# Column blocks of an input projection walked to and fro, with the turning block kept in PSUM and the order re-planned

## The chip, the cores and the metric

One core of one Trainium2 chip runs the whole program. The time is device microseconds of one execution; the kernel before has a median of 1818.54 us over three runs (1816.66 to 1821.82).

## The reference: one hybrid attention and RG-LRU layer

A layer of width 4096 works on 256 latent tokens (`x`) and 256 context tokens (`ctx`), all in float32. Cut to what matters here:

```python
shift, scale, gate = split(silu(c) @ w_ada + b_ada, 3)      # w_ada: 4096 x 12288; for c and for c_ctx
h_x = rmsnorm(x, norm_w) * (1 + scale_x) + shift_x          # the same for ctx with c_ctx
q, k, v, ga, xl, gl = split(h @ w_in)                       # w_in: 4096 x 9216
att = gqa(rope(qknorm(q)), [rope(k_x), k_ctx], [v_x, v_ctx])
lru = sum over 2 directions of an RG-LRU scan of conv(xl), the context scanned first
x + gate * (concat(rmsnorm(att) * silu(ga), rmsnorm(lru) * silu(gl)) @ w_out)   # w_out: 4096 x 4096
```

Only the latent stream is returned, so of the context only k, v and xl are needed.

## The kernel before: stages, groups and the planned order

**Numbers.** A product of two float32 matrices is made of three TensorE passes: each operand is split into a rounded part `hi` and a rest `lo`, and `hi*hi + hi*lo + lo*hi` is summed in PSUM. For a weight that means a load of 512 KB into one of six `raw` buffers (SP issues these loads, L298), a cast to `hi` on ScalarE (ACT, L646) and a subtraction to `lo` on VectorE (DVE, L650), which frees the raw buffer.

**First stage (to about 747 us).** Everything that both token streams need: column blocks `k`, `v`, `l0` to `l3` of w_in, 512 columns each, against 32 tiles of 128 rows of w_in (k-tiles). The h of a k-tile exists only after the modulation of its 128 channels is known, and this needs the whole height of w_ada for these columns. So the k-tiles are taken in 11 groups of 1, 1, 2, 2, 2, 4, 4, 4, 4, 4, 4 (`FIRST`, `groups`). In a group, `group_pieces` goes through the six blocks in the same order each time; of a block there are four tiles (latent or context, two halves of tokens), each summed in one of four PSUM banks `pm` over the k-tiles of this group. At a block's end `accum_task` moves the four tiles to accumulators in SBUF: a copy on DVE in group 0 (L693), an add on DVE afterwards (L695). That makes 24 evictions a group. Group 0 runs its blocks twice, first for the latent tokens, then for the context.

`mod_tasks` computes shift and scale of the next group's channels, for both c and c_ctx. Its loads of w_ada go to one of two engines by quads (four of the 32 rows a partition holds): TensorE with 32 output rows (L485), or DVE, a multiply-add for each row and vector (L473, L475), summed over partitions at the end by two small matmuls (`fold`, L498). `MOD_V` says how many of eight quads of shift and of scale are DVE's; in the groups of four k-tiles it is none of the shift's and seven of the scale's, in the small groups none. `coeff_tasks` and `prep_tasks` then scale, transpose (L597), modulate (ACT, L607 and L608) and split h (DVE, L617).

**Around it.** The start loads x in eight slices (`load_stream`, L364), whose squares ACT sums (L385); then w_ada for group 0, then ctx. Small parameters and the rope tables come through POOL's DMA queue: `load_params` (L373 to L380) fills rows of one tile `par`, cleared by one memset (L333), and `rope_tasks` (L433 to L443) loads the cosine and sine table into a slot `u`, the broadcast norm weight into `rope` (two DMAs at L435, eight at L440), and multiplies them. `params(1, 2)` transposes the late parameters and `decay` makes the LRU's decay from them with some 25 small DVE instructions (L410 to L424). After the first stage come the query blocks with attention, the two gates beside 16 LRU heads (conv, gates L1227 to L1229, scans L1270 and L1271), and the output projection; DVE sums w_ada for the output gate (L846) along the way, and l0 to l3 are spilled to DRAM through POOL (L893).

**The order.** Each engine runs its instructions in the order in which the program issues them. That order is made at build time by `Plan`: a task has a list of engines with costs, dependencies, PSUM and SBUF slots to take and give, a place in the main chain (`pos`) and often a place before which it may not start (`nb`). `order` simulates the engines with those costs and issues whatever could start first, by `pos` where several could. `LAT` is the lag between engines; a load is reckoned at 1.3 us before it, `LOAD` = 1.6 us for it and `LOAD_LAT` = 0.5 us after. A wait that the plan doesn't know stops an engine, and all behind it. DMAs that depend on nothing start as soon as their queue gets to them, whatever their place in the plan.

## Time and profile before

| | us |
|---|---|
| median of three runs | 1818.54 |
| the profiled execution: its time | 1821.06 |
| its span | 1819.2 |
| busy: PE / DVE / ACT / POOL | 1732.4 / 1419.1 / 854.8 / 68.0 |
| first main matmul (L738) starts | 41.6 |
| last group of the first stage starts | 677.7 |
| mean HBM traffic over the span | 247 GB/s |

PE is TensorE, SP the engine that issues the loads. PE's busy time is modelled, since its matmuls overlap, so a busy PE is not yet a PE at its peak; waits and their releasers tell more. An answer by windows gives busy us of each engine in a stretch, with the number of its instructions, the granted share of TensorE's clock, the busy share of the 16 DMA engines and the traffic. Groups 0, 1, 4 and 6 of the first stage start their main matmuls at 41.6, 76, 208.7 and 353.4 us.

### The profile page before, as it was taken

To read this page: it belongs to the slowest core of one execution; us is meant where nothing else is said; L and a number is where in the kernel's file an instruction comes from. 1 tells how busy PE (TensorE), PEld (TensorE's weight loads), DVE (VectorE), ACT (ScalarE), POOL (GpSimd) and SP (SyncE) were. 2 spreads that over 40 slices of the span, in tenths; PEclk is the share of its full clock that TensorE was granted. 3 is DMA by queue.
4 is the path that set the end of the run, shared out by engine and by line. 5 is a ranking of instruction groups with operands and counts; after the bars stand their busy time and mean duration, and the time that the engine had idled before them with its cause. 6 is when DMAs were issued, how large, how long until landed. Compare 5 with 4: busy or idle time off the path is not lost.

```text
span 1819.2 us, 25705 instructions
## 1 busy us (share of the span) xinstructions
PE 1732.4 (95%) x9709; PEld 1386.6 (76%) x9709; DVE 1419.1 (78%) x2000; ACT 854.8 (47%) x1258; POOL 68.0 (4%) x111
## 2 busy tenths in 40 slices
PE   2989989999999999999999999999999999999998
PEld 1556646676767677887777899999999988888887
DVE  1665988998989797556799778987996997777774
ACT  4422221323323133367776866758667643333332
POOL 2000000000000000200000000000000000000000
PEclk9999999999999999999999999999999999999999
DMA  9989988788886975863466447765875798989893
GB/s 284 337 277 309 323 307 297 259 269 278 280 297 226 329 244 175 248 197 116 141 206 223 148 125 240 243 204 174 278 251 159 220 322 298 313 296 315 300 307 117
DMA packets 286331, 451.80 MB, mean 248 GB/s; under 512 B 15136, under 2 KB 122512, under 8 KB 285696
## 3 DMA queue, kind: packets, MB, share of 16 engines
q1 hardware_dynamic: 279392, 428.43, 71.8%
q0 software_dynamic: 6816, 21.74, 4.0%
q8 instruction: 76, 1.25, 0.3%
q14 instruction: 47, 0.39, 0.1%
HBM read 441.72 MB, written 8.39 MB: 247 GB/s over the span
## 4 chain that ended last, share of the span: by engine, by line
issue 43%; PE 39%; DVE 12%; ACT 3%; DMA 2%; POOL 0%; DVEq 0%; ACTq 0%; POOLq 0%
PE pm L915 8%; PE pm L916 8%; PE pm L914 8%; DVE lo L650 4%; PE pm L939 4%; PE pm L938 4%; PE pm L940 4%; DVE ga L846 2%; PE po L1104 1%; ACT hi L646 1%; DVE h L1270 1%; DVE h L1271 1%; PE pe L1066 1%; DVE u L1204 1%; PE pt L1090 1%
## 5 line engine op out<-in xcount | busy, mean ns | idle before, releaser
L646 ACT CAST hi<-raw 128x1024 fp32r<-128x1024 f32 x416 | 435.7, 1048 | 716.8 <-PE pm L740 336.9
L650 DVE TENSOR_TENSOR lo<-raw,hi 128x1024 fp32r<-128x1024 f32 x416 | 506.9, 1221 | 165.2 <-ACT hi L646 162.4
L738 PE MATMUL pm<-hi,h 128*128 128x512 f32 x768 | 316.5, 412 | 10.9 <-DVE a L695 8.7
L914 PE MATMUL pm<-hi,h 128*128 128x512 f32 x768 | 308.5, 402 | 0.0
L740 PE MATMUL pm<-hi,h 128*128 128x512 f32 x768 | 302.2, 394 | 3.5 <-DVE h L617 3.5
L739 PE MATMUL pm<-lo,h 128*128 128x512 f32 x768 | 302.0, 393 | 0.8 <-DVE lo L650 0.8
L915 PE MATMUL pm<-lo,h 128*128 128x512 f32 x768 | 299.7, 390 | 1.6 <-DVE lo L650 1.6
L916 PE MATMUL pm<-hi,h 128*128 128x512 f32 x768 | 299.4, 390 | 0.0
L938 PE MATMUL pm<-h,hi 128*128 128x256 f32 x1024 | 293.7, 287 | 0.0
L940 PE MATMUL pm<-h,lo 128*128 128x256 f32 x1024 | 290.7, 284 | 0.8 <-DVE lo L650 0.8
L939 PE MATMUL pm<-h,hi 128*128 128x256 f32 x1024 | 290.2, 283 | 0.0
L738 PEld LDWEIGHTS pm<-hi,h 128*128 128x128 f32 x768 | 145.4, 189 | 104.0 <-issue 41.0
L695 DVE TENSOR_TENSOR a<-pm,a 128x512 f32<-128x512 f32 x240 | 159.4, 685 | 67.9 <-PE pm L740 67.9
L939 PEld LDWEIGHTS pm<-h,hi 128*128 128x128 f32 x1024 | 197.0, 192 | 1.7 <-issue 0.7
L938 PEld LDWEIGHTS pm<-h,hi 128*128 128x128 f32 x1024 | 196.9, 192 | 1.7 <-issue 0.7
L940 PEld LDWEIGHTS pm<-h,lo 128*128 128x128 f32 x1024 | 196.8, 192 | 1.4 <-DVE lo L650 1.4
L846 DVE SCALAR_TENSOR_TENSOR ga<-raw,sc,ga 128x512 f32<-128x512 f32 x248 | 185.8, 749 | 8.1 <-DMA raw<-in_w_ada_dram 3.2
L740 PEld LDWEIGHTS pm<-hi,h 128*128 128x128 f32 x768 | 145.5, 189 | 36.0 <-DVE h L617 3.9
L915 PEld LDWEIGHTS pm<-lo,h 128*128 128x128 f32 x768 | 144.4, 188 | 35.0 <-DVE lo L650 3.5
L914 PEld LDWEIGHTS pm<-hi,h 128*128 128x128 f32 x768 | 144.3, 188 | 31.3 <-issue 3.1
L916 PEld LDWEIGHTS pm<-hi,h 128*128 128x128 f32 x768 | 144.1, 188 | 30.4
L739 PEld LDWEIGHTS pm<-lo,h 128*128 128x128 f32 x768 | 145.7, 190 | 27.2 <-DVE lo L650 1.3
(191 smaller groups left out, 1700.7 us busy)
## 6 DMA issues: line engine op xcount, KB each, us to landing
raw<-in_w_ada_dram SPq DMA_DIRECT2D x384, 512.0 KB, 5.5
raw<-in_w_in_dram SPq DMA_DIRECT2D x288, 512.0 KB, 4.8
raw<-in_w_out_dram SPq DMA_DIRECT2D x128, 512.0 KB, 5.3
h<-in_x_dram SPq DMA_DIRECT2D x8, 512.0 KB, 8.8
h<-in_ctx_dram SPq DMA_DIRECT2D x8, 512.0 KB, 10.7
xl_d<-a POOLq DMA_DIRECT2D x4, 1024.0 KB, 6.7
xin<-xl_d POOLq DMA_DIRECT2D x16, 256.0 KB, 4.6
a<-in_x_dram POOLq DMA_DIRECT2D x8, 512.0 KB, 6.7
```

The lines of the kernel that those rows point to most:

```text
L646: S.copy(d["hi"], raw)
L650: V.tensor_tensor(out=d["lo"], in0=d["raw"], in1=d["hi"].bitcast(F32), op=ALU.subtract)
L738: T.matmul(ps[s, t], hi, wh, start=f, stop=False)
L739: T.matmul(ps[s, t], hi, wl, start=False, stop=False)
L740: T.matmul(ps[s, t], lo, wh, start=False, stop=e)
L846: V.scalar_tensor_tensor(out=d["acc"], in0=w[:, i], scalar=s_, in1=d["acc"], op0=ALU.mult, op1=ALU.add)
L914: T.matmul(ps[t], hi, wh, start=f, stop=False)
L915: T.matmul(ps[t], hi, wl, start=False, stop=False)
L916: T.matmul(ps[t], lo, wh, start=False, stop=e)
L938: T.matmul(o, wh, hi, start=f, stop=False, skip_group_check=True)
L939: T.matmul(o, wh, lo, start=False, stop=False, skip_group_check=True)
L940: T.matmul(o, wl, hi, start=False, stop=e, skip_group_check=True)
```

## The change

Odd groups go through the blocks backwards, so the last block of a group is the first of the next. Its four tiles are not evicted at that turn; the sum goes on in the same four PSUM banks (at the first turn only the context's two tiles, since the latent ones were done earlier). The first eviction of each of the 24 tiles is now a copy on ACT instead of DVE. `MOD_V` gives DVE two and three of the scale's quads in groups 3 and 4 (none before), five in group 5 (seven before). `load_params` runs behind a memset of its two rows of `par` at 0.6 of a unit after the first main matmul, and the key's rope loads behind a one-element memset of `rope`, in the last group instead of the third, the table last. The planner's lags are by engine, its loads by packet size, and a scan is reckoned at twice 0.66 us instead of twice 0.34.

```diff
@@ -32,17 +32,19 @@
...
 TP = 2
-LAT = 0.15
+LAT = dict(P=0.2, A=0.14, D=0.14, S=0.15)
 TABLE = 1.3
...
 AHEAD = 18.0
-LOAD = 1.600
-LOAD_LAT = 0.5
+LOAD = {512: 1.62, 1024: 1.50}
+LOAD_REST = 1.44
+LOAD_LAT = 2.2
 GATE_HEAD = 0.0
...
 LRU_CHUNKS = 10.2
-MOD_V = (0, 7)
+MOD_V = {3: (0, 2), 4: (0, 3), 5: (0, 5)}
+MOD_V_REST = (0, 7)
 FIRST = (1, 1, 2, 2, 2)
...
 MOD_RATE = 13.0
@@
+def load_time(load):
+    return LOAD.get(4 * load[0][-1], LOAD_REST)
...
@@ -124,8 +131,8 @@
...
         for i, l in enumerate(t.loads):
-            dma = max(dma, raw[i] + 1.3) + LOAD
-            s = max(s, dma + LOAD_LAT)
+            dma = max(dma, raw[i] + LOAD_LAT) + load_time(l)
+            s = max(s, dma + 0.06)
         return s, dma, s0
     def fixed(self, tasks):
...
@@ -330,7 +337,7 @@
...
     V.memset(ones_c, 1.0)
-    V.memset(par, 0.0)
+    V.memset(par[:, 0], 0.0)
     S.activation(tnh, cin, AF.Tanh, scale=0.5)
     V.scalar_tensor_tensor(out=tnh, in0=tnh, scalar=1.0, in1=cin, op0=ALU.add, op1=ALU.mult)
@@ -430,7 +437,7 @@
...
             d["tab"] = slot("u", [128, 2, 2, 128])
-            Q.dma_start(d["tab"].rearrange("p t f d -> p (t f d)"), consts[:, 130:642])
+            V.memset(rope[:, 0, 0, 0:1], 0.0)
             for t in range(2):
...
                 rv = rope[:, t, 1].rearrange("p (a h f) -> p a h f", a=2, h=2)
@@ -438,6 +445,7 @@
...
                         Q.dma_start(rv[:, a, h], wv[:, a, 1 - h].to_broadcast([128, 32]))
+            Q.dma_start(d["tab"].rearrange("p t f d -> p (t f d)"), consts[:, 130:642])
         def mul():
             V.tensor_tensor(out=rope, in0=rope, in1=d["tab"], op=ALU.mult)
@@ -447,7 +455,7 @@
         return add(mul, [("D", dve(512))], [a], pos, rel=["u"])
-    def mod_tasks(k0, nk, out_, p0, p1, nb, cl):
+    def mod_tasks(k0, nk, out_, p0, p1, nb, cl, on_v=(0, 0)):
         n = 128 * nk
@@ -455,7 +463,7 @@
...
         d = {}
-        v_of = [[(quads * (2 * i + 1)) // (2 * on_v) for i in range(on_v)] for on_v in (MOD_V if nk == G else (0, 0))]
+        v_of = [[(quads * (2 * i + 1)) // (2 * m) for i in range(m)] for m in on_v]
         p_of = [[q for q in range(quads) if q not in v] for v in v_of]
...
         last_p = [(part, p[-1]) for part, p in enumerate(p_of) if p][-1]
@@ -684,15 +692,14 @@
...
         return accs[name]
-    def accum_task(name, fn, dep, pos):
+    summed = {}
+    def accum_task(name, tile_, fn, dep, pos):
         acq = ["a8"] if name not in acc_last else []
-        acc_last[name] = add(fn, [("D", dve(512))], [dep, acc_last.get(name)], pos, acq=acq, rel=["pm"])
-    def accum(a, ps, k0):
-        if k0 == 0:
-            V.tensor_copy(a, ps)
-        else:
-            V.tensor_tensor(out=a, in0=ps, in1=a, op=ALU.add)
+        ops = [("D", dve(512))] if (name, tile_) in summed else [("A", act(512))]
+        deps = [dep, summed.get((name, tile_)), acc_last.get(name)]
+        acc_last[name] = summed[name, tile_] = add(fn, ops, deps, pos, acq=acq, rel=["pm"])
     BLOCKS = [("k", C_K), ("v", C_V)] + [(f"l{i}", C_XL + 512 * i) for i in range(4)]
     groups = [(sum(FIRST[:i]), n) for i, n in enumerate(FIRST)]
@@ -700,57 +707,75 @@
...
     group_parts = []
-    for (k0, nk), p in zip(groups, starts):
+    for gi, ((k0, nk), p) in enumerate(zip(groups, starts)):
         parts, i = [], 0
+        order_ = BLOCKS[:: -1 if gi % 2 else 1]
         if nk == 1:
             for b in range(0, 6, 2):
-                u = unit(w_in[0], k0, 1, BLOCKS[b][1], 1024, p + U1 * i)
-                parts += [[(u, k0, 1, 0, False)], [(u, k0, 1, 512, True)]]
+                c0 = min(c for _, c in order_[b : b + 2])
+                u = unit(w_in[0], k0, 1, c0, 1024, p + U1 * i)
+                for e in range(2):
+                    parts.append((order_[b + e][0], [(u, k0, 1, order_[b + e][1] - c0, e == 1)]))
                 i += 1
         else:
-            for _, c1 in BLOCKS:
+            for name, c1 in order_:
                 us = []
...
                     i += 1
-                parts.append(us)
+                parts.append((name, us))
         group_parts.append(parts)
+    carried = {}
     def group_pieces(gi, ss, free):
...
         tiles = [(s, t) for s in ss for t in range(2)]
-        for (name, _), parts in zip(BLOCKS, group_parts[gi]):
+        for ib, (name, parts) in enumerate(group_parts[gi]):
             ps = {}
+            olds = {i: carried.pop(i) for i in tiles if ib == 0 and i in carried}
+            hold = free and ib == len(BLOCKS) - 1 and gi + 1 < len(groups)
             for ip, (u, kk, n, cc, whole) in enumerate(parts):
                 for s, t in tiles:
-                    def mms(s=s, t=t, u=u, kk=kk, n=n, cc=cc, ip=ip, ps=ps, np_=len(parts)):
+                    old = olds.get((s, t))
+                    def mms(s=s, t=t, u=u, kk=kk, n=n, cc=cc, ip=ip, ps=ps, np_=len(parts), old=old, hold=hold):
                         if ip == 0:
-                            ps[s, t] = bank("pm")
+                            ps[s, t] = bank("pm") if old is None else old[s, t]
                         tk = slice(128 * t, 128 * t + 128)
...
                             hi, lo = (x_[:, k, tk] for x_ in (hx, hc)[s][g])
-                            f, e = ip == 0 and i == 0, ip == np_ - 1 and i == n - 1
+                            f, e = old is None and ip == 0 and i == 0, not hold and ip == np_ - 1 and i == n - 1
                             T.matmul(ps[s, t], hi, wh, start=f, stop=False)
...
                             T.matmul(ps[s, t], lo, wh, start=False, stop=e)
-                    def done(s=s, t=t, name=name, ps=ps):
-                        accum(acc_tile(name)[:, 2 * s + t], ps[s, t], k0)
-                        drop(ps[s, t])
                     end = free and whole and (s, t) == tiles[-1]
-                    last = end and name == "l3" and ip == len(parts) - 1
+                    last = end and ib == len(BLOCKS) - 1 and ip == len(parts) - 1
                     rel = [lambda g=k0 // G: hc[g]] if last and (k0 + nk) % G == 0 else []
                     deps = [units[u]["low"]] + [prepared[kk + i, s] for i in range(n)]
-                    p = piece(mms, mm(512, 3 * n), pos, deps, u if end else None, ["pm"] if ip == 0 else [], rel)
+                    p = piece(mms, mm(512, 3 * n), pos, deps, u if end else None, ["pm"] if ip == 0 and old is None else [], rel)
                     pos += mm(512, 3 * n)
                     if ip == len(parts) - 1:
-                        accum_task(name, done, p, pos)
+                        if hold:
+                            carried[s, t] = ps
+                        else:
+                            def done(s=s, t=t, name=name, ps=ps, first=(name, (s, t)) not in summed):
+                                a = acc_tile(name)[:, 2 * s + t]
+                                if first:
+                                    S.copy(a, ps[s, t])
+                                else:
+                                    V.tensor_tensor(out=a, in0=ps[s, t], in1=a, op=ALU.add)
+                                drop(ps[s, t])
+                            accum_task(name, (s, t), done, p, pos)
     weights_of_groups = plan.tasks[:]
@@ -786,7 +811,6 @@
...
         loaded[1, g] = pre(lambda g=g: load_stream(1, g), [("S", 1.456)], acq=["h4"])
-    p_late = pre(load_params, [("S", 0.3)])
     stat_tasks(0)
...
     prefix += mod0[5:]
@@ -800,8 +824,11 @@
...
     prep_tasks(*groups[0], (1,), coeff0, rstds, -40, 0.1)
-    t = add(lambda: (params(1, 2), decay()), [("P", 0.3), ("D", 1.0), ("A", 0.3, "exp"), ("D", 2.5)], [p_late], starts[2], nb=starts[1] + 1, acq=["pe"], rel=["xin", "pe"])
-    k_rope = rope_tasks(k_norm_w, starts[2], [t])
+    t = add(lambda: V.memset(par[:, 1:3], 0.0), [("D", 0.2)], [], U1 * 0.6)
+    p_late = add(load_params, [("S", 0.3)], [t], U1 * 0.6)
+    t = add(lambda: (params(1, 2), decay()), [("P", 0.3), ("D", 1.0), ("A", 0.3, "exp"), ("D", 2.5)], [p_late], starts[2] - 2, nb=starts[1] + 1, acq=["pe"], rel=["xin", "pe"])
+    k_rope = rope_tasks(k_norm_w, starts[-2] + 8, [t])
     spans = {}
...
     for gi in range(len(groups) - 1, 0, -1):
@@ -814,7 +841,7 @@
...
             m0, m1 = spans[gi + 1]
-            ends = mod_tasks(*nxt, rows, max(m0, MOD_FIRST), max(m1, MOD_FIRST), None, ("pt", "po")[gi % 2])
+            ends = mod_tasks(*nxt, rows, max(m0, MOD_FIRST), max(m1, MOD_FIRST), None, ("pt", "po")[gi % 2], MOD_V.get(gi + 1, MOD_V_REST if nxt[1] == G else (0, 0)))
             cf = coeff_tasks(*nxt, rows, ends, m1 + 0.5)
...
         if gi == 0:
@@ -1316,7 +1343,7 @@
...
         a = add(mul, [("D", dve(1024))], [a, ti], at(0.7))
-        a = [add(lambda r=r: scan(r), [("D", dve(256, 2))], [a], at(0.75 + 0.05 * r)) for r in range(2)]
+        a = [add(lambda r=r: scan(r), [("D", dve(570, 2))], [a], at(0.75 + 0.05 * r)) for r in range(2)]
         a = add(both, [("D", dve(256))], a, at(0.9), acq=["a8"] if n % 8 == 0 else [], rel=["h4"] * 3 + ["lh"])
...
```

## Rows read from the trace of the kernel before

**Rows 1.** The chain that ended last, from the page: shares of the span by engine.
```profile
issue 43%; PE 39%; DVE 12%; ACT 3%; DMA 2%; POOL 0%; DVEq 0%; ACTq 0%; POOLq 0%
```
**Rows 2.** Windows: stretch, its us, busy of PE, PEld, DVE, ACT, POOL, PEclk, DMA share, GB/s.
```profile
41.60:76.00 34.40, 30.95 (x240) 19.71 (x240) 22.57 (x38) 20.02 (x53) 0.00 (x0) 0.95 1.07 336
76.00:208.70 132.70, 126.92 (x796) 78.16 (x792) 91.09 (x163) 34.20 (x54) 0.00 (x0) 0.97 0.92 305
208.70:353.40 144.70, 132.73 (x621) 86.98 (x618) 133.28 (x200) 39.85 (x60) 0.00 (x0) 0.99 0.85 289
353.40:677.70 324.30, 319.82 (x1498) 227.85 (x1497) 282.70 (x414) 92.50 (x132) 0.00 (x0) 1.00 0.83 278
```
**Rows 3.** Waits of SP, 200 to 353 us: releaser, us in total, times, longest.
```profile
SPq L298 <- DVE u L475: 52.6, 23, 3.6
```
**Rows 4.** Waits of PE, 41 to 200 us.
```profile
PE pt L485 <- DMA raw<-in_w_ada_dram: 4.1, 5, 1.3
PE pm L740 <- DVE h L617: 3.5, 1, 3.5
```
**Rows 5.** Waits of PE, 200 to 353 us.
```profile
PE pm L738 <- DVE a L695: 6.5, 8, 1.5
PE po L485 <- DMA raw<-in_w_ada_dram: 4.2, 1, 4.2
```
**Rows 6.** Waits of PE, 353 to 747 us.
```profile
PE po L485 <- DMA raw<-in_w_ada_dram: 2.4, 4, 1.0
PE pm L738 <- DVE a L695: 2.2, 3, 1.7
```
**Rows 7.** Waits of PE, 747 us to the end.
```profile
PE pe L1228 <- DVE lo L1220: 10.0, 6, 2.5
PE pt L1090 <- DVE tp L1084: 5.7, 9, 1.1
PE pt L1039 <- DVE tp L974: 4.0, 3, 1.8
```
**Rows 8.** Windows around the start of group 0 and around three drops of the clock.
```profile
40.00:48.00 8.00, 5.60 (x13) 4.09 (x14) 5.72 (x7) 7.97 (x20) 0.00 (x0) 1.00 1.05 392
...
110.00:120.00 10.00, 6.52 (x21) 4.58 (x23) 6.21 (x20) 2.85 (x6) 0.00 (x0) 0.66 0.69 240
234.00:240.00 6.00, 4.05 (x12) 1.16 (x13) 5.86 (x10) 0.00 (x0) 0.00 (x0) 0.72 0.94 339
1193.00:1199.00 6.00, 3.89 (x16) 3.41 (x17) 3.97 (x7) 3.36 (x5) 0.71 (x1) 0.72 0.89 285
```
**Rows 9.** Timeline of POOL: the first of ten rope issues (start us, us).
```profile
11.04 0.54 POOL L435 DMA_DIRECT2D rope<-in_k_norm_w_dram  x1
```
**Rows 10.** Timeline of ACT: first, fourth and last arrival of an x slice.
```profile
6.87 0.63 ACT L385 ACTIVATE tp<-h 128x512 f32<-128x512 f32 x1 [0.49 <-DMA h<-in_x_dram]
...
11.91 0.63 ACT L385 ACTIVATE tp<-h 128x512 f32<-128x512 f32 x1 [0.43 <-DMA h<-in_x_dram]
...
22.27 0.63 ACT L385 ACTIVATE tp<-h 128x512 f32<-128x512 f32 x1 [3.29 <-DMA h<-in_x_dram]
```
**Rows 11.** Source line 973: min, median and max ns, first and last start us.
```profile
L973 DVE TENSOR_TENSOR a<-a,rope x2: 691/692/692, 705.6 to 708.6; 128x512 f32<-128x512 f32 x2
```
**Rows 12.** Groups of instructions: busy us, mean ns of one, idle before.
```profile
L695 DVE TENSOR_TENSOR a<-pm,a 128x512 f32<-128x512 f32 x240 | 159.4, 685 | 67.9 <-PE pm L740 67.9
L693 DVE COPY a<-pm 128x512 f32<-128x512 f32 x24 | 16.2, 690 | 8.8 <-PE pm L740 8.8
L475 DVE SCALAR_TENSOR_TENSOR xin<-raw,sc,xin 128x512 f32<-128x512 f32 x162 | 121.4, 749 | 13.5 <-DMA raw<-in_w_ada_dram 10.3
L505 ACT COPY tp<-pt 128x512 f32<-128x512 f32 x3 | 1.8, 587 | 9.4 <-PE pt L498 9.4
L1271 DVE TENSOR_TENSOR_SCAN h<-h,h,h 128x256 f32<-128x256 f32 x32 | 24.0, 751 | 1.1
```
**Rows 13.** Timeline of PE: one quad of w_ada for four k-tiles.
```profile
227.74 1.07 PE L485 MATMUL pt<-raw,wg 128*32 128x512 f32 x8
```

More of the change, by code (lines that the diff above doesn't have):

```diff
@@ L110, in estimate @@
         for d in t.deps:
-            s = max(s, d.end + (0.0 if d.ops[-1][0] == t.ops[0][0] else self.LAT))
+            s = max(s, d.end + (0.0 if d.ops[-1][0] == t.ops[0][0] else self.LAT[d.ops[-1][0]]))
         need = {}
@@ L137, in fixed @@
             while started and queue and self.raw:
-                u, _ = queue.pop(0)
+                u, l = queue.pop(0)
                 self.raw.sort()
-                self.dma = max(self.dma, self.raw.pop(0) + 1.3) + LOAD
-                u.arrived = (u.arrived or []) + [self.dma + LOAD_LAT]
+                self.dma = max(self.dma, self.raw.pop(0) + LOAD_LAT) + load_time(l)
+                u.arrived = (u.arrived or []) + [self.dma + 0.06]
             s, dma, _ = self.estimate(t)
@@ L193, in put @@
             self.t[e] = s
-            s += self.LAT
-        t.end = s - self.LAT
+            s += self.LAT[e]
+        t.end = s - self.LAT[t.ops[-1][0]]
         if t.ops[0][0] == "S":
```

## The prediction

> **What bounds the kernel now.** I read five views, from wide to narrow. The chain that ended last [rows 1] consists of TensorE (PE) and its issue to 82%, of DVE to 12%: PE sets the end, and only its stops can be won. Such shares average over stages, so next I cut the span where groups of w_in rows begin [rows 2]. The reader should see three limits there. Up to 208.7 us (groups 0 to 3) the DMA share is 1.07 and 0.92: transfers bind. From 208.7 to 353.4 us (groups 4 and 5) DVE is busy 133.28 of 144.70 us, 92%, and the DMA share falls to 0.85: DVE binds, and through it the transfers, since SP, which issues the loads, waits 52.6 us there for DVE to empty raw buffers [rows 3]. From 353.4 us on PE is busy 319.82 of 324.30 us. Fourth come PE's own waits [rows 4 to 7]: 4.1 us for w_ada and 3.5 us for one late DVE subtraction before 200 us; 6.5 us for bank evictions and 4.2 us for w_ada from 200 to 353 us; 2.4 and 2.2 us of the same two kinds up to 747 us; then 10.0, 5.7 and 4.0 us in the late stage, the 10.0 at the LRU gate matmuls. Fifth, the granted clock [rows 8]: behind the longer stops it falls from 2.4 to 1.2 GHz. A mean of 0.66 over 10 us costs 3.4 us, one of 0.72 over 6 us costs 1.7 us; a second drop like the last one follows in the LRU stage. The stops listed, with their clock, are some 50 us. The rest of the span is PE's own work, which the change hardly touches.
>
> **The change part by part.** The sum is made against the profiled execution, 1821.06 us (span 1819.2), which is 2.5 us above the median of the three runs, 1818.54.
>
> *The key rope loads leave the start.* Nothing holds these ten POOL DMAs (and the table's) back today; they begin at 11 us [rows 9]. ACT's waits show x slices landing at 6.87 and, three slices later, at 11.91 us [rows 10]: 1.68 us each. The eighth should land at 6.87 + 7 x 1.68 = 18.6 us; it lands at 22.27, 3.7 us late, and all loads up to the first main matmul queue behind it. Value -3.7; bounds 0 (something else held the slice) and -5.2 (three slices' time, if the w_ada loads behind were slowed as well). They go to a main position 12 planned us ahead of the last group, so to about 660 us. The DMA share there is 0.83 [rows 2], which hides them: 0, or +3.7 without that cover. They now wait for a DVE memset, and behind them on POOL stand only the spills of l0 to l3, which wait for the last group's evictions. The keys' rotation needs the table at 705.6 us [rows 11], some 45 us after. The eight parameter loads move behind a memset as well, 27 planned us ahead of PE's transposes of them: 0; the two memsets are one short DVE instruction each.
>
> *First evictions on ACT.* 24 copies of 690 ns, 16.6 us, leave DVE; ACT pays about 587 ns each [rows 12], 14.1 us. Twelve fall where ACT is busy 7.97 of 8 us with the statistics of the context [rows 8]: 7.0 us that could hold up its rstd, and with it the second half of group 0. Bounds 0 and +7.0. I take +2, nearer to 0, since transfers bind this stretch (1.07) [rows 2] and PE has w_ada matmuls to do meanwhile.
>
> *Turning blocks.* 11 groups evict 24 tiles each today: 24 copies and 240 adds. At the first turn 2 and at nine more turns 4 tiles stay in PSUM: 38 adds x 685 ns [rows 12] = 26.0 us less on DVE. *Fewer w_ada quads on DVE for group 5* (5 for 7): 2 x 8 operations x 749 ns [rows 12] = 12.0 us less, and 2 x 1.07 us [rows 13] more on PE. Both meet where DVE binds: 12.0 us and two to three turns (8 to 12 adds, 5.5 to 8.2 us) off 133.28 leave about 114 of 144.70 us, 79%, under the 87% (282.70 of 324.30) of the stretch behind it, whose waits are small [rows 2, 6]. The waits from 200 to 353 us are 6.5 + 4.2, with 1.7 us of clock: 12.4. I take -10, net of the 2.1 that PE pays. Bounds -12.4 and +2.1. What is late next there is w_ada by its own transfer, as before 200 us.
>
> *w_ada quads on DVE for groups 3 and 4* (2 and 3 of 8): 5 x 8 operations at about half of 749 ns are 15 us on a DVE that is busy 91.09 of 132.70 us [rows 2]: covered. PE loses five quads of half of 1.07 us and gains two folds. DVE holds such a load 8 x 0.37 = 3 us, where PE frees it in half a us, and this is where transfers bind. Value 0, bounds -3 and +5.
>
> *Decay.* PE's 3.5 us wait [rows 4] and 3.4 us of clock [rows 8] near 110 us came from a subtraction that stood on DVE behind the decay's many small operations. The same operations stay, planned 2 us earlier. Value 0, bounds -7 and +7.
>
> *The order elsewhere.* The planner's durations come nearer to the trace: one of a scan's two instructions takes 751 ns [rows 12]; it reckoned 0.34, now 0.66. From 353 to 747 us the waits are under 5 us: -2, bounds -5 and +5. The three late waits are 19.7 us, and two clock drops 3.4: I take -4, bounds -13 (the LRU gates and their clock) and +10, since a new order of 16 heads can place as many stops as it removes.
>
> *Holding the turning block* has a cost that no row shows: all four banks stay full over the turn. The rows speak for 0: no other piece is queued for these banks, and over 66 block ends PE waited 11 times for an eviction, 8.7 us in all [rows 5, 6]. The Trainium skill, "PSUM — Partial Sum Buffer", section "Summary: rules for kernel authors", says to evacuate promptly, because the space is tight, and so speaks against this change. By that rule each of ten turns would cost a wait like those, 8.7/11 = 0.8 us, and the sum would be 8 us higher.
>
> Sum: -3.7 + 2 - 10 + 0 + 0 - 2 - 4 = -17.7. The profiled execution becomes 1803.4, the median 1800.8; forecast **1801**.
>
> **The rivals.**
> (a) *DVE was covered after all, 1815.* Evictions hold PE for 8.7 us in 700; if the freed DVE time is spent waiting for w_ada, only the start's 3.7 us stay. For it: the DMA share is 0.85 even where DVE binds. Against it: SP's 52.6 us of waits for DVE [rows 3]. 0.13.
> (b) *Larger, 1778.* All waits before 747 us (22.9) and those at the LRU gates (10.0) go, with their clock (8.5) and the start's 3.7; ACT and PE pay 4: -41. For it: they are few and have names. Against it: a fixed order always leaves some. 0.11.
> (c) *Slower, 1848: PE's order runs ahead of the loads.* The planner reckons 1.44 to 1.62 us a load, before 1.60. In the bound stretches 0.524 MB at 305 and 289 GB/s [rows 2] take 1.72 and 1.81 us. PE takes its instructions in order, so a w_ada matmul placed too early stops the main matmuls behind it; one such stop was 4.2 us and 1.7 us of clock [rows 5, 8], 5.9 together. It decides from (17.7 + 5.5)/5.9, four stops more than today; eight, about one a group, give 47 - 18 = +29. Against it: the lag before and after a load was raised from 1.8 to 2.3 us, so a single load is reckoned later than before. 0.11.
> (d) *The turn costs a bank wait*, ten times the mean of today's, 0.8 us: 1809. For it: four banks, all held. Against it: nothing else wants them. 0.04. This is what the PSUM page's rule would do.
> (e) *The change doesn't do what it says, 1818*: memsets placed so early that the loads still run at the start, tiles evicted as often. Against it: the counts above follow from the code. 0.03.
>
> **How the numbers follow.** The forecast has 0.58. About 0.3%, 5.5 us, is what a measurement of this kernel can tell from no change: faster is under 1813.1, slower over 1824. Faster: the forecast but for 0.01, (b), (d) and 0.02 of (a), 0.74. Same: the rest of (a), (e) and that 0.01, 0.15. Slower: (c), 0.11. The bounds of all terms reach from 1773 to 1866, but they don't all fall on one side. The range of 1783 to 1820 holds the forecast's spread, (a), (d), (e) and some of (b); it leaves out (c) and the rest of (b), under 0.2.
>
> **What the profile after would show.** Ten rope issues on POOL near 660 us, the eighth x slice near 18.6 us, the first main matmul near 38 us for 41.6. 202 adds on DVE and 24 copies on ACT. Groups 4 and 5 in about 135 us for 144.7, DVE under 85% there, SP's wait for the w_ada products well under 52 us, no clock drop at 235 us. Against me: PE waits for w_ada above 20 us (c), evictions' waits right behind turns (d), groups that all start about 4 us earlier and no more (a), a second half of group 0 that starts 5 us late on ACT.

## The result, and the profile after

After: 1807.28 us, the median of 4 runs (1806.90 to 1807.69); before, beside it, 1817.60 us, the median of 4 (1815.77 to 1821.82). The ratio is 0.994, with a 95% interval of 0.9922 to 0.9958: faster by more than 0.3%, by about 10 us where 17.7 were forecast. The time lies inside the range. The sum that led there does not stand: three of its terms were far off, in both directions, and that the total came out near is luck.

The page of after, with its busy times, and the chain that ended last, which answers to [rows 1]:

```profile
span 1805.5 us, 25645 instructions
...
PE 1736.0 (96%) x9693; PEld 1388.1 (77%) x9693; DVE 1383.2 (77%) x1965; ACT 865.0 (48%) x1282; POOL 67.8 (4%) x111
...
PE 73%; DVE 14%; DMA 5%; ACT 4%; issue 3%; SPq 1%; POOL 0%; DVEq 0%; ACTq 0%; POOLq 0%
```

PE still sets the end. To see where its time went I cut both traces at the first main matmul of each group and of each later stage: the query blocks, the columns of the two gates `ga` and `gl` (L938 before, L965 after), the output projection. All times are us:

| stretch | before | after | difference |
|---|---|---|---|
| start to the first main matmul | 41.6 | 35.6 | -6.0 |
| groups 0 to 3 | 167.2 | 173.8 | +6.6 |
| groups 4 and 5 | 144.6 | 126.1 | -18.5 |
| groups 6 to 8 | 246.4 | 250.4 | +4.0 |
| group 9 | 77.9 | 87.8 | +9.9 |
| group 10 | 67.2 | 67.3 | +0.1 |
| query blocks 0 and 1 | 117.6 | 124.5 | +6.9 |
| from there to the gate columns | 145.0 | 141.2 | -3.8 |
| gate columns, both halves | 446.6 | 433.4 | -13.2 |
| output projection to the end | 365.1 | 365.4 | +0.3 |

The rows add up to -13.7, the difference of the spans (1819.2 and 1805.5). Some 41 us were won and 28 given back. The windows of after over the same stretches answer to [rows 2]; the last row is the stage of the gate columns, for which the same view of before stands in the second fence (columns as in [rows 2]):

```profile
35.60:73.80 38.20, 33.28 (x248) 19.85 (x248) 7.81 (x16) 31.83 (x76) 3.92 (x8) 0.91 1.10 337
73.80:209.40 135.60, 130.42 (x777) 77.10 (x776) 104.69 (x198) 33.94 (x54) 0.00 (x0) 0.97 0.96 323
209.40:335.50 126.10, 124.73 (x594) 86.97 (x592) 110.14 (x166) 40.08 (x60) 0.00 (x0) 1.00 0.81 280
335.50:673.70 338.20, 327.66 (x1513) 230.96 (x1512) 279.47 (x406) 92.32 (x132) 5.86 (x11) 0.98 0.82 278
1006.70:1440.10 433.40, 428.90 (x3379) 416.20 (x3378) 375.84 (x495) 310.40 (x416) 20.93 (x29) 1.00 0.66 210
```

```profile
1007.50:1454.10 446.60, 433.37 (x3380) 418.52 (x3379) 378.74 (x498) 311.53 (x416) 21.00 (x29) 0.99 0.65 205
```

The reader should see three things. In groups 4 and 5 PE is busy 124.73 of 126.10 us: DVE binds no longer, though it is still at 87%. From 335.5 to 673.7 us PE has 10.5 us without work where before it had 4.5 of 324.30. In the stage of the gate columns PE's idle time fell from 13.2 to 4.5 us with the same matmuls.

PE's waits of after (line waiting, releaser, us in total, times, longest), from 41 to 200 us, from 200 to 336, from 640 to 865 and from 865 to the end, answer to [rows 4 to 7]:

```profile
PE pm L755 <- ACT a L773: 4.1, 3, 2.0
PE pm L757 <- DVE h L625: 3.7, 1, 3.7
...
PE pm L755 <- DVE a L775: 0.8, 2, 0.5
...
PE pm L755 <- DVE a L775: 10.1, 2, 8.4
PE pm L942 <- DVE lo L658: 7.5, 1, 7.5
...
PE pe L1255 <- DVE lo L1247: 3.1, 4, 1.5
PE pt L1117 <- DVE tp L1111: 1.8, 4, 0.8
PE pt L1066 <- ACT hi L654: 1.1, 1, 1.1
```

The last three lines wait at the same three places as those of [rows 7], moved by 27 lines, the last of them now for ACT: 6.0 us for 19.7. Two stops of 8.4 and 7.5 us are new, near 660 and 770 us. The timeline of after shows what stands in front of the first of them (start us, us, engine, line, operation; in brackets the idle time of the engine before it and what ended it):

```profile
650.98 0.06 DVE L440 MEMSET rope<- 128x1 f32 x1
651.35 0.57 POOL L442 DMA_DIRECT2D rope<-in_k_norm_w_dram  x1 [607.43 <-DVE rope L440]
...
658.70 0.54 POOL L448 DMA_DIRECT2D u<-in_shape_consts_dram  x1 [0.97 <-DMA rope<-in_k_norm_w_dram]
...
662.33 0.69 DVE L451 TENSOR_TENSOR rope<-rope,u 128x512 f32<-128x512 f32 x1 [11.28 <-DMA u<-in_shape_consts_dram]
662.93 0.68 DVE L775 TENSOR_TENSOR a<-pm,a 128x512 f32<-128x512 f32 x1
...
663.67 0.80 PE L755 MATMUL pm<-hi,h 128*128 128x512 f32 x1 [8.42 <-DVE a L775]
```

DVE runs the memset, and its next instruction is the product of the key's rope with its table, which needs all eleven loads. They take from 651.35 to 662.33 us. DVE takes its instructions in order, so the evictions queued behind the product wait 11.28 us too, the banks fill, and PE stops for 8.42 us. The first matmul after the stop takes 0.80 us. The query's rope does the same 100 us later (the releaser named is the next load on POOL's queue, issued right behind the table's):

```profile
757.49 0.06 DVE L440 MEMSET rope<- 128x1 f32 x1
...
769.74 0.69 DVE L451 TENSOR_TENSOR rope<-rope,u 128x512 f32<-128x512 f32 x1 [12.19 <-DMA wg<-in_lru_wa_dram]
...
771.62 0.80 PE L942 MATMUL pm<-lo,h 128*128 128x512 f32 x1 [7.54 <-DVE lo L658]
```

### The profile page after: what moved, and what is told of

It reads as the page before. It is cut to its first block, busy times and chain, and to the rows that moved or that the text cites. A ratio compares the mean times of both kernels' runs of the same rounds, so it can differ in the third digit from the quotient of the medians.

```text
span 1805.5 us, 25645 instructions
## 1 busy us (share of the span) xinstructions
PE 1736.0 (96%) x9693; PEld 1388.1 (77%) x9693; DVE 1383.2 (77%) x1965; ACT 865.0 (48%) x1282; POOL 67.8 (4%) x111
## 4 chain that ended last, share of the span: by engine, by line
PE 73%; DVE 14%; DMA 5%; ACT 4%; issue 3%; SPq 1%; POOL 0%; DVEq 0%; ACTq 0%; POOLq 0%
PE pm L755 8%; PE pm L942 8%; PE pm L943 8%; PE pm L941 8%; PE pm L757 7%; PE pm L756 7%; PE pm L965 6%; PE pm L966 6%; PE pm L967 6%; DVE lo L658 4%; DMA raw<-in_w_ada_dram 3%; PE pt L493 2%; PE po L493 2%; DVE ga L873 2%; DVE a L775 1%
## 5 line engine op out<-in xcount | busy, mean ns | idle before, releaser
L965 PE MATMUL pm<-h,hi 128*128 128x256 f32 x1024 | 293.7, 287 | 0.0
L965 PEld LDWEIGHTS pm<-h,hi 128*128 128x128 f32 x1024 | 196.2, 192 | 2.2 <-issue 1.2
L941 PEld LDWEIGHTS pm<-hi,h 128*128 128x128 f32 x768 | 144.6, 188 | 31.8 <-issue 3.6
L775 DVE TENSOR_TENSOR a<-pm,a 128x512 f32<-128x512 f32 x202 | 132.6, 683 | 32.4 <-PE pm L757 32.1
```

Source lines behind the costliest of these rows:

```text
L941: T.matmul(ps[t], hi, wh, start=f, stop=False)
L965: T.matmul(o, wh, hi, start=f, stop=False, skip_group_check=True)
```

## The experiments

A row of the table above is meant where I write of a stretch; "after" is the changed kernel. The diffs of the first eight experiments below are against it, of the next two against the kernel before, of the last two against it again. All ratios are to the kernel before on the same chip.

**The rope products held back.** The loads may start 20 planned us ahead of `pos`, the product now 6 ahead of it, so 14 behind them. The theory: the product's place on DVE, right behind its loads, makes both late stops.

```diff
-        return add(mul, [("D", dve(512))], [a], pos, rel=["u"])
+        return add(mul, [("D", dve(512))], [a], pos, nb=pos - 6, rel=["u"])
```

> The changed kernel with the two rope products planned at least 14 planned us behind their loads; all else keeps its place. Theory: the changed kernel gives back what it won because DVE stops 11.3 us at 651 us and 12.2 us at 758 us for the rope table, which now is loaded last and behind a memset, and PE stops behind it for 8.4 and 7.7 us, with 5.1 and 3.4 us of clock. All of this goes: 1807 - 24.6 = 1783 us, no clock drop at 659 or 768 us, and the last group starts near 660 us (673.7 in the changed kernel). Rival: PE's later work would have waited anyway (transfers, other DVE work), and little comes through to the end: 1800 us or more.

1788.81 us, ratio 0.9823 (0.9798 to 0.9848). The span is 17.7 us shorter than after's: group 9 takes 77.9 us again (-9.9) and the query blocks 115.0 (-9.5). The key's product now stands 17 us behind its memset, and still waits 3.79 us for the table:

```profile
654.00 0.06 DVE L440 MEMSET rope<- 128x1 f32 x1
671.32 0.69 DVE L451 TENSOR_TENSOR rope<-rope,u 128x512 f32<-128x512 f32 x1 [3.79 <-DMA u<-in_shape_consts_dram]
```

The stops came from the product's place. Without them the change gives 31.4 us of span (13.7 + 17.7); with them more than half of that was lost.

**Loads at the start again, product late.** This takes the memsets away that hold the rope loads and the late parameters back, from the kernel of the last experiment. The table is not among what moves: it is loaded last, into the `u` buffer, which the w_ada products hold until then, and is issued at 639.84 us.

```diff
-            V.memset(rope[:, 0, 0, 0:1], 0.0)
+            pass
...
-    V.memset(par[:, 0], 0.0)
+    V.memset(par, 0.0)
...
-    t = add(lambda: V.memset(par[:, 1:3], 0.0), [("D", 0.2)], [], U1 * 0.6)
+    t = add(lambda: None, [("D", 0.2)], [], U1 * 0.6)
```

> The kernel of the run before, but without the memsets that hold the key rope and the parameter loads back, so that they run at the start again; the order is the same. Theory: their packets delayed the last x slice and everything behind it. First main matmul near 41.6 us (35.6 with late loads), but transfers bind up to 208 us and the lead had shrunk to 2.2 us by group 1 and to nothing by group 4, so at the end 0 to 3 us slower than the run before. Rival: the start's lead is kept to the end: 6 us slower than the run before. Second rival: it was the order and not the loads that made the start shorter: first main matmul at 36 us again.

1792.75 us, ratio 0.9843 (0.9819 to 0.9867). The first main matmul starts at 38.7 us for 35.2, and the last x slice comes later than in after; the two rows are ACT's, of after and of this kernel:

```profile
17.47 0.63 ACT L392 ACTIVATE tp<-h 128x512 f32<-128x512 f32 x1
```

```profile
20.07 0.63 ACT L392 ACTIVATE tp<-h 128x512 f32<-128x512 f32 x1 [1.11 <-DMA h<-in_x_dram]
```

So these loads, the table not counted, are worth 3.5 us at the first matmul, of the 6.0 by which after is earlier. Of these 3.5 us, 2.0 are left at group 4, 1.4 at group 10 and 0.6 of the span. The medians differ by 3.9, with ratios whose intervals overlap: whether the start's gain lasts to the end stays open.

**First evictions on DVE.** The 24 copies go back from ACT to DVE, the rest as in after.

```diff
-        ops = [("D", dve(512))] if (name, tile_) in summed else [("A", act(512))]
+        ops = [("D", dve(512))]
...
-                                    S.copy(a, ps[s, t])
+                                    V.tensor_copy(a, ps[s, t])
```

> The changed kernel with the 24 first evictions as copies on DVE again, in the plan too. Theory: on ACT they collided with the statistics of the context; PE waited 4.1 us for them and the clock fell once more (6.8 us, 3.4 lost). Group 1 starts some 5 us earlier than in the changed kernel (69 us for 73.8), and as transfers bind up to 208 us, 0 to 3 us of it arrive at the end: 1804 to 1807 us. Rival: all of it arrives: 1800 us. Second rival: DVE is the scarcer engine there: group 1 no earlier, 1807 us or slower.

1803.50 us, ratio 0.9905 (0.9881 to 0.9929), span 4.9 us shorter; group 1 starts at 71.5 us for 73.8. PE's wait for ACT's copies (4.1 us in after) is gone. Copies on ACT cost some 4 to 5 us (3.8 by the medians, 4.9 by the spans); I had reckoned 2.

**Product late and copies on DVE together.** The edits of the first and third experiments.

> The changed kernel with both repairs: rope products 14 planned us behind their loads, and the first evictions on DVE again. Theory: the two act in different stretches and add up: 17.7 us of span from the first and 4.9 from the second off 1805.5, so a span near 1783 and a median near 1785, the fastest of all. Rival: the 4.9 us of the second came from another place in the order by chance and do not add: 1788 to 1790.

1785.39 us, ratio 0.9826 (0.9809 to 0.9842); the span, 1780.0, is 25.5 us shorter than after's, where 17.7 and 4.9 were won alone. But this profiled execution is the fastest of its four. The median lies 3.4 us under that of the first experiment, and the two ratios, 0.9826 and 0.9823, do not differ: that the two gains add up is likely, and not shown.

**Evicting the turning block.** Everything else stays, but the block at a turn is evicted and summed like the others.

```diff
-            hold = free and ib == len(BLOCKS) - 1 and gi + 1 < len(groups)
+            hold = False
```

> The changed kernel with no tile held over a turn: the blocks still run to and fro, but all 264 tiles are evicted. Theory: the 38 adds, 26 us of DVE, are worth something only where DVE binds. Groups 4 and 5 took 126.1 us in the changed kernel and 144.6 before; without the held turns they take 129 to 133 us, the other groups 0 to 2 us more in all, and the total grows by 4 to 8 us, to 1811 to 1815. Rival: the fewer quads of group 5 did it alone: groups 4 and 5 stay within 2 us of 126, the total within 3 us of 1807.

1811.85 us, ratio 0.9967 (0.9955 to 0.9979), span 5.3 us longer. Groups 4 and 5 take 130.4 us for 126.1, with ten more instructions on DVE:

```profile
209.60:340.00 130.40, 126.90 (x594) 87.05 (x593) 116.68 (x176) 40.33 (x61) 0.00 (x0) 1.00 0.80 274
```

Holding the block is worth some 5 us, nearly all of it where DVE bound before.

**The quads of w_ada as before.** Groups 3 to 5 get the numbers of quads on DVE that they had before.

```diff
-MOD_V = {3: (0, 2), 4: (0, 3), 5: (0, 5)}
+MOD_V = {}
```

> The changed kernel with the quads of w_ada as before: seven of group 5's scale on DVE, none of groups 3 and 4. Theory: group 5's two quads, 12 us of DVE, are the larger half of the relief in groups 4 and 5: these take 134 to 138 us for 126.1; groups 1 to 3 get 2 to 3 us shorter, as DVE holds no loads for groups 3 and 4 there (135.6 us in the changed kernel, 132.8 before). Total +6 to +9: 1813 to 1816. Rival: the held turns did it: groups 4 and 5 within 3 us of 126, and the total falls to 1805.

1806.86 us, ratio 0.9934 (0.9920 to 0.9949). Groups 4 and 5 take 127.7 us (+1.6), groups 1 to 3 131.3 for 135.6 (-4.3), the span is 0.9 us shorter. My theory fell, and the whole edit gives nothing. But this takes two things back at once. Without the products of groups 3 and 4 in front of them, DVE's w_ada products for group 5 start at 114 us instead of 162, so what its two quads are worth alone stays open.

**The scan reckoned short again.**

```diff
-        a = [add(lambda r=r: scan(r), [("D", dve(570, 2))], [a], at(0.75 + 0.05 * r)) for r in range(2)]
+        a = [add(lambda r=r: scan(r), [("D", dve(256, 2))], [a], at(0.75 + 0.05 * r)) for r in range(2)]
```

> The changed kernel with a scan reckoned at 2 x 0.34 us again instead of 2 x 0.66. Theory: the right duration of the scans is what made the stage of the gates and LRU heads shorter by 13 us (from the first gate matmul to the first output matmul: 446.6 us before, 433.4 after), as PE's waits for the gates' lo went from 10.0 us to nearly nothing, with two clock drops. It comes back: 446 us for the stage and about 1820 us in all. Rival: the lags and load times of the planner did it: the stage stays within 3 us of 433 and the total within 4 us of 1807.

1828.72 us, ratio 1.0042 (1.0028 to 1.0056): slower than the kernel before. The stretch to the gate columns takes 146.4 us (141.2 in after), the gate columns 447.5 (433.4). The LRU's gate matmuls wait for DVE as they did in [rows 7]:

```profile
PE pe L1255 <- DVE lo L1247: 9.9, 6, 2.4
```

**The planner's old lags and load times.** Two of the changed lines:

```diff
-LOAD_REST = 1.44
-LOAD_LAT = 2.2
+LOAD_REST = 1.6
+LOAD_LAT = 1.3
```

with the lags of 0.15 us for every engine, no load times by size, and 0.5 us behind a load, as before.

> The changed kernel with the planner's lags and load times as before (0.15 us between any two engines; 1.3 us ahead of a load, 1.6 for it, 0.5 behind). Theory: they matter little: groups 4 and 5 stay within 4 us of 126.1, the stage of the LRU heads within 3 us of 433, the total within 5 us of 1807. Rival: the right load times are what brought DVE's products for w_ada forward: groups 4 and 5 take 136 us or more, and the total is 1816 or more.

1804.95 us, ratio 0.9929 (0.9910 to 0.9948): in the total no difference, as the theory had it (the profiled execution, at 1810.50, is the slowest of its four). But groups 4 and 5 take 138.6 us for 126.1, as the rival had it. Group 5 issues 88 w_ada matmuls where after issues 64, and PE waits there for evictions:

```profile
PE pm L755 <- DVE a L775: 6.6, 5, 1.9
```

Groups 6 to 8 give 5.1 us back, and the rope's stop falls into group 10 (74.4 us for 67.3) instead of 9. One edit moves work between groups and the stop with it, so in the total this tells neither apart: inconclusive. For groups 4 and 5 it says that without the new times most of their gain is gone, though the loads are moved and the turns held.

**The scan's reckoning alone, in the kernel before.** The edit of the scan line, with 570 in place of 256, and nothing else of the change.

> The kernel before, with one change alone: a scan is reckoned at 2 x 0.66 us instead of 2 x 0.34. Theory: this edit of the plan is worth by itself what its removal cost the changed kernel (22 us of span): from the third query block to the output projection 591.6 us before become about 574, PE's 10.0 us of waits at the LRU gates fall below 4, both clock drops there go, and the total is 1800 to 1806. Rival: it helps only with the new lags and load times: within 5 us of 1819.

1800.32 us, ratio 0.9904 (0.9889 to 0.9919). From the third query block to the output projection 574.3 us for 591.6, and the wait at the gates falls from [rows 7]'s 10.0 us:

```profile
PE pe L1228 <- DVE lo L1220: 2.6, 4, 1.2
```

This one number is worth 17 us, and alone it beats the whole change.

**The late loads alone, in the kernel before.** The key's rope loads (with the table) behind a memset and late, their product held back as above, and the parameters' task 2 planned us earlier; the parameters' loads stay at the start.

```diff
+            V.memset(rope[:, 0, 0, 0:1], 0.0)
...
-        return add(mul, [("D", dve(512))], [a], pos, rel=["u"])
+        return add(mul, [("D", dve(512))], [a], pos, nb=pos - 6, rel=["u"])
...
-    t = add(lambda: (params(1, 2), decay()), [("P", 0.3), ("D", 1.0), ("A", 0.3, "exp"), ("D", 2.5)], [p_late], starts[2], nb=starts[1] + 1, acq=["pe"], rel=["xin", "pe"])
-    k_rope = rope_tasks(k_norm_w, starts[2], [t])
+    t = add(lambda: (params(1, 2), decay()), [("P", 0.3), ("D", 1.0), ("A", 0.3, "exp"), ("D", 2.5)], [p_late], starts[2] - 2, nb=starts[1] + 1, acq=["pe"], rel=["xin", "pe"])
+    k_rope = rope_tasks(k_norm_w, starts[-2] + 8, [t])
```

> The kernel before with three edits alone: the key's rope loads in the last group (behind a memset), their product 14 planned us behind them, and the parameters' task two planned us earlier. Both free a buffer that DVE's products for w_ada need: the rope table held u, the parameters xin. Theory: in the kernel before these products start at 178.9 us and crowd DVE in groups 4 and 5; in the changed kernel they start at 116.4 us although nothing else calls for it, and that is what shortened groups 4 and 5. Here they start before 150 us, groups 4 and 5 fall from 144.6 to 126 to 134 us, the first main matmul comes 3 us earlier, and the total is 1801 to 1808. Rival: it takes the held turns and the copies on ACT: groups 4 and 5 stay above 140 us, the total within 5 us of 1815.

1804.51 us, ratio 0.9926 (0.9907 to 0.9944). The span is 14.2 us shorter than before's, about as much as the whole change gave. The first main matmul starts at 35.4 us for 41.6, and at group 4 this lead is still there: 202.0 us for 208.8. Groups 4 and 5 take 137.2 us, between the two theories' figures: 7.4 of the 18.5 us. The source line of the w_ada products on DVE (min, median and max ns, first and last start), first before, then this kernel, then after:

```profile
L475 DVE SCALAR_TENSOR_TENSOR xin<-raw,sc,xin x162: 740/751/754, 178.9 to 653.1; 128x512 f32<-128x512 f32 x162
```

```profile
L476 DVE SCALAR_TENSOR_TENSOR xin<-raw,sc,xin x162: 739/751/754, 116.1 to 638.5; 128x512 f32<-128x512 f32 x162
```

```profile
L483 DVE SCALAR_TENSOR_TENSOR xin<-raw,sc,xin x172: 476/751/755, 116.4 to 626.4; 128x512 f32<-128x512 f32 x154, 128x256 f32<-128x256 f32 x18
```

These products are built up in a `u` and a `xin` buffer. Before, the rope table stood in a `u` buffer from the start to its product at 115.80 us, and the parameters in a `xin`. With the table late and the parameters done earlier, DVE's first w_ada product starts 63 us sooner here. After's 116.4 us is not the same thing, though my theory took it for that: its products up to 160 us are the 128x256 ones of groups 3 and 4, which the change itself gives to DVE, and those for group 5 begin at 162 us:

```profile
162.29 0.49 DVE L481 TENSOR_SCALAR xin<-raw,sc 128x512 f32<-128x512 f32 x1 [1.08 <-PE po L506]
```

In groups 4 and 5 this line keeps DVE busy for 77.72 us before, 69.40 here and 58.32 in after: part of the work now lies in front, in stretches in which DVE is not full. Shown is that these edits together bring the early start and 7.4 us in groups 4 and 5; that it goes through the two buffers is read from the code. Why the first product stood as late as 178.9 us when the table's buffer was free at 116, the trace doesn't tell, and each edit alone was not tried.

**The fastest found.** Product late, copies on DVE, and `MOD_V = {}`.

> Both repairs (rope products later, first evictions on DVE) and the quads of w_ada as before; the decay reckoned as in the changed kernel. Theory: without quads for groups 3 and 4 on DVE, groups 1 to 3 take some 131 us (134 with them and both repairs), and the median is 1780 to 1783, the fastest of all. Rival: the quads are worth nothing either way once DVE's products start early: the median stays within 2 us of 1785, as it did when the decay's price was mended too.

1781.70 us, ratio 0.9805 (0.9791 to 0.9820), the fastest of all; its page:

```profile
span 1779.4 us, 25669 instructions
...
PE 1725.0 (97%) x9709; PEld 1384.8 (78%) x9709; DVE 1392.8 (78%) x1965; ACT 853.5 (48%) x1258; POOL 67.8 (4%) x111
```

Groups 1 to 3 take 131.1 us for 133.9 with the change's quads, but the interval overlaps that of the kernel with product and copies alone: the quads' part isn't settled.

**The same with the decay reckoned longer** (5.5 us of DVE in place of 2.5).

> The version with both repairs (rope products later, first evictions on DVE), and two more edits: the quads of w_ada as before, and the decay reckoned at 5.5 us of DVE instead of 2.5, which the trace shows as some 6.5. Theory: groups 1 to 3 get 2 to 4 us shorter without the quads of groups 3 and 4, as they did in the changed kernel, and PE's wait of 3.3 us near 108 us with its clock drop goes: a median of 1778 to 1783. Rival: these few us are within what any new order does by chance: 1784 to 1789.

1783.90 us, ratio 0.9813 (0.9797 to 0.9829). Groups 1 to 3 take 134.0 us, and the clock still falls near 106 us. Nothing is won.

## Why the prediction was right, and where it failed

The sign and the range were right; the likeliest case held only in the total, and by luck: 17.7 us of stops for the rope tables stood against 8.5 and 13.0 us more than forecast in groups 4 and 5 and in the late stage. By the prediction's own terms:

**The start, -3.7 and +2.** The loads' part has the right mechanism: the last x slice starts at 17.47 us (18.6 forecast, 22.27 in [rows 10]). Its size is nearer to -6. The 3.5 us of the second experiment leave the table out, and with it the kernel before gains 6.2 at the first main matmul (41.6 to 35.4; one trace each, and a kernel whose loads did not move starts at 40.0). But group 4 of after starts at 209.4 us for 208.8: all of it is given back in groups 0 to 3. Two terms take it: the copies on ACT, put at +2 (without them group 4 starts at 206.1), and the next one.

**The quads of groups 3 and 4, 0.** I called these products covered, because DVE had time. Groups 1 to 3 take 131.3 us for 135.6 without the quads' edits, inside my bound of +5, and group 4 starts at 204.3. With the copies on DVE as well it starts at 202.4, in the fastest kernel.

**Groups 4 and 5, -10.** The place was right, and so was the wait: PE's idle time there fell from 12.0 to 1.4 us and one clock drop of 1.7 us is gone, 12.3 together, close to the bound of -12.4. What makes it 18.5 is work: the w_ada matmuls take 6.2 us less there, and 5.6 us more in groups 6 to 8. The windows are of that line, busy us of PE and PEld, first before, then after:

```profile
208.80:353.40 144.60, 23.25 (x140) 3.29 (x136) 0.99 0.85 289
353.40:599.80 246.40, 30.64 (x200) 4.61 (x200) 1.00 0.82 275
```

```profile
209.40:335.50 126.10, 17.08 (x112) 2.57 (x112) 1.00 0.81 280
335.50:585.90 250.40, 36.20 (x216) 5.84 (x216) 1.00 0.81 280
```

Which edit freed DVE is less clear. Undone alone in after, the held turns cost 4.3 us there, all the quads' edits 1.6 and the planner's new times 12.5; the late loads alone, in the kernel before, brought 7.4. That is more than 18.5, so these parts overlap, and of them my sum had only the turns and the quads. That the moved loads let DVE's w_ada products start earlier I did not see: I had costed the moves as transfers and instructions and never asked which buffers they hold. The new times alone, in the kernel before, were not tried. Of the signs named in advance, no clock drop at 235 us came true, DVE's share under 85% did not (87%), and SP's wait fell less than "well under 52":

```profile
SPq L305 <- DVE u L483: 40.9, 16, 4.2
```

**The rope loads' new place: the step that failed.** I wrote "0, or +3.7 without that cover", named the DMA share as the cover, and counted 45 us to the keys' rotation. The transfers were indeed hidden; the instruction that waits for them was not. I asked who needs the table (the rotation), and not where its product stands in DVE's order: `("S", 2.0)` gives the loads 2 planned us, 4.2 with what the plan adds in front and behind, and they take 11. It cost 17.7 us, by the first experiment. The prediction moved the DMAs on POOL's queue, and left out the DVE instruction that moves with them.

**Groups 6 to 9, -2, beside that.** Groups 6 to 8 became 4.0 us longer, and the same groups of the kernel with the late product take 252.0 us, so the rope is not the reason. It is work, by the windows above: 16 w_ada matmuls more, 5.6 us, while PE's idle time fell from 4.3 to 2.1 us. With the planner's old times groups 4 and 5 have 148 of these matmuls and groups 6 to 8 only 200, and take 245.3 us.

**The late stage, -4.** The mechanism is right (DVE's scan under-reckoned, PE's waits, the clock behind them) and the term is mis-sized: -3.8 and -13.2, 17.0 in all, past my own bound of -13. The three waits of [rows 7] fell by 13.7 us, to 6.0, and both clock drops, 3.4 us, went: 17.1. I had all of these rows and took a fifth of them, for fear that a new order makes as many stops as it removes. Both the scan edit alone (-17.3 in these stretches) and its undoing (+19.3) show that the one number carries it.

**Decay, 0.** Right: the wait is there in after, 3.7 us, and so is the clock's fall, as is told below.

**Holding the turning block, 0.** Right, and better than that. PE waits for DVE's evictions 0.8 us in all from 200 to 336 us. The Trainium skill, "PSUM — Partial Sum Buffer", section "Summary: rules for kernel authors", says to evacuate promptly. This trace does not bear it out for a block whose sum goes on and whose banks nobody else wants: evicting at the turns made the span 5.3 us longer.

**The rivals.** Waits for w_ada did not grow (c): 1.5 us up to 200 us and 0.5 up to 336, for 4.1 and 4.2 in [rows 4, 5]. No bank wait stood behind turns (d). DVE was not covered (a): groups 4 and 5 gained. The larger gain (b), 1778, was cut off by the rope's product and ACT's copies: with both put right it is 1785.39. A slower outcome was possible through a mechanism that I had not named: without the scan's number the change is slower than before, at 1828.72.

## What to carry to other kernels

When a load is moved, follow the first instruction that consumes it, not the one that needs the final value: on an engine that runs in order its wait stops everything queued behind it. Give such a load the duration that the trace shows from its first issue to its last landing, in the planner too. And list the buffers that a moved step holds, from first write to last read: releasing one early may be worth as much as the transfer itself (7.4 and 6.2 us here; that the 7.4 came through the buffers is not shown). Before any of this, hold each planned duration against the trace: the scan's, 0.34 us for a measured 0.75, was worth 17 us alone.

## What I had not expected of the hardware

Eleven small loads (ten of the norm's weights, and the table) took 11.0 us in after, from the first issue at 651.35 us to the product at 662.33. Eleven issues of 0.55 us would be 6. In the kernel with the late product it was 16.9 us, from 654.37 to 671.32, of which DVE waited 3.79: even 14 planned us between the loads and their product were not enough there.

The stops cost more than their length. Windows of after around four falls of the granted clock, to answer [rows 8]:

```profile
46.00:56.00 10.00, 7.68 (x60) 4.51 (x61) 0.76 (x3) 8.94 (x27) 0.00 (x0) 0.66 1.17 288
104.00:114.00 10.00, 6.33 (x43) 3.21 (x43) 7.96 (x29) 3.37 (x6) 0.00 (x0) 0.78 0.89 293
659.00:670.00 11.00, 6.33 (x18) 5.09 (x19) 7.19 (x13) 4.81 (x9) 0.24 (x1) 0.53 0.43 108
768.00:776.00 8.00, 4.38 (x14) 3.59 (x15) 4.10 (x4) 0.69 (x1) 2.16 (x3) 0.57 0.60 187
```

In the third of them the granted clock stood at 1.2 GHz from 659.1 us for 10.2 us: it fell during the 8.42 us stop, and 5.6 us of it lie behind the stop's end at 663.67, which by its half clock costs some 2.8 us more. In the fourth it stood there from 768.3 us for 6.8 us; 3.5 us of it lie behind the stop, 1.7 us more. Stop and clock together, 11.2 and 9.2 us, are about the 9.9 and 9.5 us that the later product gave back. The first two falls stand at PE's waits for ACT's copies and for the subtraction behind the decay, which are half as long or less, and these too were at that level for 6.8 us each. The two drops of before in the stage of the gate columns, 3.4 us long each, are gone in after with the waits that stood there, and came back when the scan's number was undone.
